# Diffusion step with a DeltaNet layer on one core: the early splits and the second layer's modulation tied to the first MLP's instructions

## The chip, the cores and the metric

The kernel runs on one core of one Trainium2 chip. The metric is the device time of one execution in microseconds (us); lower is better. TensorE is called PE below, VectorE DVE, ScalarE ACT, GpSimd POOL and SyncE SP; SP computes nothing here, its queue issues most of the transfers (DMAs).

## The reference, cut to what matters

Two layers run over 128 context tokens and 512 latent tokens that share the weights: an attention layer and a gated DeltaNet layer. Each is followed by an MLP, and each norm is modulated by vectors that are themselves a product of a condition with a weight matrix:

```python
def modulation(cond, w_mod, b_mod):
    m = jax.nn.silu(cond) @ w_mod + b_mod              # (1024) @ (1024, 6144), per layer and per group
    return jnp.split(m[..., None, :], N_MOD, axis=-1)
def trunk_layer(x, mods, gain1, gain2, w1, w2, mixer):
    shift1, scale1, gate1, shift2, scale2, gate2 = mods
    mix, aux = mixer(rms_norm(x, gain1) * (1 + scale1) + shift1)
    x = x + gate1 * mix
    h = rms_norm(x, gain2) * (1 + scale2) + shift2
    x = x + gate2 * (jnp.square(jax.nn.relu(h @ w1)) @ w2)   # (1024 -> 4096 -> 1024)
    return x, aux
def delta_mixer(h, ...):
    proj = h @ w_in                                    # q, k, v, z: 8 heads of 128 columns each
```

All of it is float32. The kernel makes a product of two float32 matrices from three faster products: each operand is split into a high part (a rounded copy) and a low part (what the rounding left), and high times high, high times low and low times high are added.

## The kernel before, in words

Activations lie transposed, features on the partitions: eight tiles of 128 features by 640 tokens. A dense layer goes through its weight matrix in blocks of 128 output columns and, for each block, through two halves of 320 tokens. One block and one half are 24 matmuls of 128x320 (eight feature tiles, three products each); this unit is called a half step below. The MLP of a layer has four quarters of 8 blocks of `w1` and 8 blocks of `w2`, so 64 blocks and 128 half steps.

A block's weights come by one 512 KB transfer into a `raw` buffer (three of them, filled by SP's queue), and ACT writes the high part and DVE the low part into a pair of `wx` buffers (five pairs). The sink of a `w1` half step is a ReLU on ACT, a product on DVE, and a split on both; that of a `w2` half step is one or two adds to `x` on DVE. Results lie in five PSUM buffers until their sink has run.

While the first MLP runs (`mlp(0, ...)`), two other pieces of work are to be done beside it:

- `modulate(1, 0, ...)`, the product that gives the second layer's first shift and scale. The condition has 32 columns, and `w_mod` streams through PE in 128x512 pieces. Four of them, with `tile_position=(0, 32 * q)` for q from 0 to 3, make one of eight accumulation steps; each writes another 32 partitions of the PSUM tile `mod`. Their weights come into two `raw` buffers of 512 KB each.
- `presplit()`, which splits 29 blocks of the DeltaNet layer's input weights ahead of time. A block comes as two 256 KB pieces into `rawp` (three buffers), ACT writes the high part of a piece and DVE the low part into a pair of `w` buffers (three pairs), and two 512 KB transfers on POOL's queue write the pair to DRAM (`wd`), from where the DeltaNet layer reads it.

All of this is written as Python generators that `weave` interleaves by their numbers of steps. The order in which the engines get the instructions is not that of the code, though: a scheduler with priorities and an assumed duration for each instruction sorts them afterwards, and an instruction of low priority goes ahead wherever the scheduler believes its engine free. Each engine then works strictly in its order, and waits where an operand is missing. The last steps of the MLP (`mid2`) load and split three more pairs of `w` buffers for the DeltaNet layer's first head and normalise the first token half.

Of the kernel before, what the change touches and what calls it, by code (L numbers as in the profile page):

```python
# [15 lines left out]
P = 128  # L16
D = 1024
FT = D // P
# [59 lines left out]
def weave(*parts):  # L78
    live = [[0, n, i, g] for i, (g, n) in enumerate(parts)]
    while live:  # L80
        live.sort(key=lambda e: ((e[0] + 1) / e[1], e[2]))
        e = live[0]
        try:
            next(e[3])
            e[0] += 1
        except StopIteration:
            live.pop(0)


def drain(g):  # L90
    for _ in g:
        pass


class Model:
# [277 lines left out]
    def modulate(self, l, slab, fetch, alloc=None, early=False):  # L373
        nc = self.nc
        acc = alloc or (lambda: self.ps("mod", 1))
        ps = acc()[:, :512]
        get = lambda k: fetch(self.a["w_mod"][l, k * P : (k + 1) * P, slab * 2048 : (slab + 1) * 2048])
        ahead = get(0) if early else None
        for k in range(FT):
            views = ahead or get(k)  # L380
            ahead = get(k + 1) if early and k + 1 < FT else None
            for q in range(4):
                nc.tensor.matmul(  # L383
                    ps[32 * q : 32 * q + 32, :], self.cond[:, k, :], views[q],
                    start=k == 0, stop=k == FT - 1, tile_position=(0, 32 * q),
                )
            yield
        m = self.main("x", shape=[P, 512])
        self.act(m, ps, AF.Copy)
        pt = acc()[:, :512]  # L390
        for b in range(4):
            self.tr(pt[:, b * P : (b + 1) * P], m[:, b * P : (b + 1) * P])
        src = pt.rearrange("p (b q i) -> p q b i", b=4, q=4)
        dst = self.mods[l][:, slab * 16 : slab * 16 + 16, :].rearrange("p (q b) i -> p q b i", q=4)
        bias = self.c1[:, l * 48 + slab * 16 : l * 48 + slab * 16 + 16].rearrange("p (q b) -> p q b", q=4)
        for i in range(2):
            self.tt(dst[:, :, :, i], src[:, :, :, i], bias, ALU.add)
        if slab != 1:
            which = 0 if slab == 0 else 1
            kind = 1 if slab == 0 else 4  # L400
            n = self.c1[:, 96 + 16 * which + 8 * l : 104 + 16 * which + 8 * l]
            for g in range(2):
                self.stt(self.gains[l][which][:, :, g], self.mods[l][:, kind * FT : kind * FT + FT, g],
                         self.one_col, n, ALU.add, ALU.mult)
        yield
# [9 lines left out]
    def fetch_mixed(self, src):  # L415
        r = self.raw([P, 2, 512])
        self.nc.sync.dma_start(out=r, in_=src[:, :1024].rearrange("p (q c) -> p q c", q=2))
        out = [r[:, 0, :], r[:, 1, :]]
        for i in (2, 3):
            t = self.main("a", shape=[P, 512])  # L420
            self.nc.sync.dma_start(out=t, in_=src[:, i * 512 : (i + 1) * 512])
            out.append(t)
        return out

    def fetch_slots(self, src):
        out = []
# [420 lines left out]
    def presplit(self):  # L847
        self.wd = {}
        todo = [(hd, kind) for hd in range(HEADS) for kind in (1, 0, 2) if hd] + [(hd, 3) for hd in range(HEADS)]
        w = self.a["dn_w_in"][0]  # L850
        HK = FT // 2

        def load(t, i):
            r = self.scr("rawp", 3, [P, HK, P])
            c = self.wcol(*t)
            self.nc.sync.dma_start(out=r, in_=w[i * HK * P : (i + 1) * HK * P, c : c + P].rearrange("(k p) c -> p k c", p=P))
            return r

        steps = [(t, i) for t in todo for i in range(2)]
        raws = [load(*x) for x in steps[:2]]  # L860
        for n, (t, i) in enumerate(steps):
            if n + 2 < len(steps):
                raws.append(load(*steps[n + 2]))
            if i == 0:
                pair = self.wtile(), self.wtile()
            ks = slice(i * HK, (i + 1) * HK)
            self.split(raws.pop(0), pair[0][:, ks, :], pair[1][:, ks, :])
            if i == 1:
                name = self.nm("wd")
                d = self.wd[t] = self.dp.tile([2, P, D], F32, tag=name, bufs=1, name=name)  # L870
                for z in range(2):
                    self.nc.gpsimd.dma_start(out=d[z], in_=pair[z].bitcast(F32).rearrange("p k c -> p (k c)"))
            yield
# [392 lines left out]
    def run(self):  # L1266
        tc, nc, a = self.tc, self.nc, self.a
# [3 lines left out]
        with psum("ps0") as self.pq:  # L1271
# [3 lines left out]
            x = []  # L1275
# [7 lines left out]
            h = self.first_norm(x, gm)  # L1283
# [3 lines left out]
        with pool("mlp0") as self.ph, psum("ps3") as self.pq:  # L1287
            self.extra = 3
            x = self.reload(self.xd)
            h = self.new_h()  # L1290
            nxt = []
# [13 lines left out]
                nxt2[:] = [self.pair(w, 0, kind * D) for kind in (1, 0, 2)]  # L1305
                self.mod_norm(x, 1, 0, h2, 0)

            weave((self.mlp(0, h, x, nxt, mid2), 128), (self.modulate(1, 0, self.fetch_raw), 13), (self.presplit(), 64))
            self.mod_norm(x, 1, 0, h2, 1)
            h = h2  # L1310
            xd = self.spill(x, nc.scalar)
# [91 lines left out]
```

## Time and profile before

| | |
|---|---|
| median of 3 runs | 1934.23 us (1922.34 to 1940.01) |
| the profiled execution's own time | 1927.58 us |
| its span, first to last instruction | 1925.6 us |
| PE busy | 1802.5 us (94%), 11981 records |
| DVE, ACT, POOL busy | 987.3, 754.1, 310.0 us |
| mean granted clock of PE | 0.976 |

Times inside the kernel are counted from the start of the span. A float32 matmul on PE leaves two records where a matmul on split operands leaves one. The first MLP's half steps run on PE from 356 to 869 us.

### The profile page before, as it was taken

To read this page: it belongs to the slowest core of one execution; us is meant where nothing else is said; L and a number is where in the kernel's file an instruction comes from. 1 tells how busy PE (TensorE), PEld (TensorE's weight loads), DVE (VectorE), ACT (ScalarE), POOL (GpSimd) and SP (SyncE) were. 2 spreads that over 40 slices of the span, in tenths; PEclk is the share of its full clock that TensorE was granted. 3 is DMA by queue.
4 is the path that set the end of the run, shared out by engine and by line. 5 is a ranking of instruction groups with operands and counts; after the bars stand their busy time and mean duration, and the time that the engine had idled before them with its cause. 6 is when DMAs were issued, how large, how long until landed. Compare 5 with 4: busy or idle time off the path is not lost.

```text
span 1925.6 us, 31049 instructions
## 1 busy us (share of the span) xinstructions
PE 1802.5 (94%) x11981; PEld 1665.9 (87%) x11981; DVE 987.3 (51%) x2293; ACT 754.1 (39%) x1725; POOL 310.0 (16%) x405
## 2 busy tenths in 40 slices
PE   6999999988799999999999999999799999999997
PEld 2777877977789999999888988776699999999997
DVE  4646663744443333455778876653645334343342
ACT  2445542543331322334756655524433223131331
POOL 2343221411100000032211111110232000000012
PEclk8899999999999999999999999999999999999998
DMA  7651147399943332233434233564622222222211
GB/s 274 219 162 35 34 131 218 103 346 346 364 126 120 100 89 76 77 99 126 138 108 117 76 97 112 162 185 150 206 64 77 77 77 75 70 76 77 77 45 55
DMA packets 289065, 248.84 MB, mean 129 GB/s; under 512 B 44847, under 2 KB 246982, under 8 KB 288918
## 3 DMA queue, kind: packets, MB, share of 16 engines
q1 hardware_dynamic: 269072, 207.85, 35.6%
q0 software_dynamic: 9136, 32.18, 4.4%
q10 hardware_dynamic: 10710, 6.83, 1.1%
q8 instruction: 94, 1.54, 0.3%
q14 instruction: 53, 0.43, 0.1%
HBM read 199.00 MB, written 45.20 MB: 127 GB/s over the span
## 4 chain that ended last, share of the span: by engine, by line
PE 67%; DVE 14%; DMA 12%; ACT 3%; issue 2%; POOL 1%; SPq 0%; ACTq 0%; POOLq 0%; DVEq 0%
PE dense L148 28%; PE pd L148 27%; DMA rawp<-in_dn_w_in 5%; PE scan L148 3%; PE big L148 2%; DMA raw<-in_mlp_w 2%; PE pd L383 1%; DVE cv L141 1%; PE mod L383 1%; DVE ptmp L135 1%; PE big L151 1%; DMA ptmp<-gmd 1%; DMA raw<-in_w_mod 1%; DVE wx L135 1%; DVE a L135 1%
## 5 line engine op out<-in xcount | busy, mean ns | idle before, releaser
L148 PE MATMUL pd<-h,w 128*128 128x320 f32 x2016 | 354.0, 320 | 12.0 <-ACT cv L138 7.5
L148 PE MATMUL dense<-a,wx 128*128 128x320 f32 x2238 | 342.4, 312 | 18.2 <-ACT a L138 12.4
L148 PEld LDWEIGHTS dense<-a,wx 128*128 128x128 f32 x2238 | 333.3, 189 | 23.4 <-ACT a L138 13.3
L148 PEld LDWEIGHTS pd<-h,w 128*128 128x128 f32 x2016 | 301.3, 190 | 37.9 <-issue 21.0
L138 ACT ACTIVATE wx<-raw 128x1024 fp32r<-128x1024 f32 x132 | 139.5, 1057 | 361.7 <-PE dense L148 184.8
L148 PE MATMUL dense<-h,wx 128*128 128x320 f32 x1776 | 266.7, 310 | 5.1 <-DVE x L141 2.6
L148 PEld LDWEIGHTS dense<-h,wx 128*128 128x128 f32 x1776 | 263.1, 189 | 5.9 <-issue 3.1
L135 DVE TENSOR_TENSOR wx<-raw,wx 128x1024 fp32r<-128x1024 f32 x127 | 158.5, 1250 | 177.5 <-ACT wx L138 177.2
L148 PE MATMUL pd<-a,wx 128*128 128x320 f32 x1284 | 197.4, 311 | 3.4 <-DVE x L141 2.6
L148 PEld LDWEIGHTS pd<-a,wx 128*128 128x128 f32 x1284 | 191.3, 189 | 7.6 <-issue 6.2
L135 POOL TENSOR_TENSOR x<-x,half 128x320 f32<-128x320 f32 x48 | 52.4, 1091 | 803.0 <-ACT half L138 795.1
L148 PE MATMUL pd<-h,wx 128*128 128x320 f32 x1008 | 155.8, 314 | 7.7 <-DVE x L141 4.0
L148 PEld LDWEIGHTS pd<-h,wx 128*128 128x128 f32 x1008 | 151.8, 192 | 11.8 <-issue 6.1
L141 DVE SCALAR_TENSOR_TENSOR x<-dense,c,x 128x320 f32<-128x320 f32 (+2 forms) x152 | 61.8, 435 | 164.5 <-PE dense L148 164.4
L138 ACT ACTIVATE a<-half 128x320 fp32r<-128x320 f32 x128 | 60.0, 470 | 107.8 <-DVE half L141 107.8
L135 DVE TENSOR_TENSOR a<-half,a 128x320 fp32r<-128x320 f32 x128 | 62.8, 492 | 63.4 <-ACT a L138 63.4
L141 DVE SCALAR_TENSOR_TENSOR cv<-cv,c,cv 128x644 f32<-128x644 f32 x84 | 78.3, 932 | 18.5 <-ACT cv L138 17.4
L141 DVE SCALAR_TENSOR_TENSOR x<-pd,c,x 128x192 f32<-128x192 f32 (+2 forms) x88 | 35.9, 437 | 92.6 <-PE pd L148 92.5
L135 DVE TENSOR_TENSOR w<-rawp,w 128x512 fp32r<-128x512 f32 x58 | 39.8, 690 | 71.0 <-ACT w L138 70.9
L138 ACT ACTIVATE w<-rawp 128x512 fp32r<-128x512 f32 x58 | 36.5, 630 | 94.5 <-DMA rawp<-in_dn_w_in 92.9
L138 ACT ACTIVATE half<-x 128x320 f32<-128x320 f32 x56 | 26.2, 468 | 107.3 <-DVE x L141 106.1
L148 PE MATMUL big<-wide,a 128*128 128x128 f32 x480 | 65.1, 283 | 0.4 <-issue 0.3
(284 smaller groups left out, 2514.1 us busy)
## 6 DMA issues: line engine op xcount, KB each, us to landing
raw<-in_mlp_w SPq DMA_DIRECT2D x128, 512.0 KB
raw<-in_w_mod SPq DMA_DIRECT2D x64, 512.0 KB
wd<-w POOLq DMA_DIRECT2D x58, 512.0 KB, 5.9
w<-wd SPq DMA_DIRECT2D x58, 512.0 KB
rawp<-in_dn_w_in SPq DMA_DIRECT2D x58, 256.0 KB
a<-in_w_mod SPq DMA_DIRECT2D x48, 256.0 KB
raw<-in_attn_w_in SPq DMA_DIRECT2D x12, 512.0 KB
x<-xs SPq DMA_DIRECT2D x16, 320.0 KB
```

The source lines that it names most:

```text
L135: (eng or self.nc.vector).tensor_tensor(out=out, in0=in0, in1=in1, op=op)
L138: self.nc.scalar.activation(out=out, in_=in_, func=func, **kw)
L141: self.nc.vector.scalar_tensor_tensor(out=out, in0=in0, scalar=s, in1=in1, op0=op0, op1=op1)
L148: self.nc.tensor.matmul(out, l, r, start=first, stop=last)
L151: self.nc.tensor.transpose(out, in_, self.ident[:n, :n])
L383: nc.tensor.matmul(ps[32 * q : 32 * q + 32, :], self.cond[:, k, :], views[q], start=k == 0, stop=k == FT - 1, tile_position=(0, 32 * q),)
```

## The change

`modulate_pieces` takes the place of `modulate(1, 0, ...)`: it loads one 128x512 piece of `w_mod` (256 KB) at a time into the `rawp` buffers, two pieces ahead, and issues one of the four column positions in each of its 32 steps; `raw` is left to the MLP. It is followed by `presplit()` in one generator, `beside()`, no longer side by side with it. `pinned` steps the MLP and lets `beside()` advance by at most 98 steps for 128 of the MLP's. After each step of `beside()`, every instruction that it issued on PE, DVE or ACT gets an ordering edge to the MLP's last instruction on the same engine, so that the scheduler may not put it ahead of that one. Transfers on SP's and POOL's queues get no edge. `beside()` has 33 steps of modulation and 58 of splitting, 91 in all.

```diff
+PINNED = tuple(getattr(mybir.EngineType, n) for n in ("PE", "DVE", "Activation"))
+def pinned(tc, main, n, side, m):
+    ...
+    for _ in main:
+        step += 1
+        for i in traced(at):
+            if i.engine in PINNED:
+                last[i.engine] = i.name
+        at = len(traced(0))
+        while done * n < step * m and next(side, True) is None:
+            done += 1
+            for i in traced(at):
+                if i.engine in last:
+                    tc.add_manual_dep(i, last[i.engine], why, reason="paced")
+            at = len(traced(0))
+    drain(side)
...
+    def piece(self):
+        return self.scr("rawp", 3, [P, FT // 2, P])
+
+    def modulate_pieces(self, l, slab):
+        ps = self.ps("mod", 1)[:, :512]
+
+        def load(n):
+            k, q = divmod(n, 4)
+            r = self.piece().rearrange("p k c -> p (k c)")
+            c = slab * 2048 + q * 512
+            self.nc.sync.dma_start(out=r, in_=self.a["w_mod"][l, k * P : (k + 1) * P, c : c + 512])
+            return r
+
+        raws = [load(n) for n in range(2)]
+        for n in range(4 * FT):
+            k, q = divmod(n, 4)
+            if n + 2 < 4 * FT:
+                raws.append(load(n + 2))
+            self.nc.tensor.matmul(
+                ps[32 * q : 32 * q + 32, :], self.cond[:, k, :], raws.pop(0),
+                start=k == 0, stop=k == FT - 1, tile_position=(0, 32 * q),
+            )
+            yield
+        yield from self.modulation(l, slab, ps, lambda: self.ps("mod", 1))
...
-            weave((self.mlp(0, h, x, nxt, mid2), 128), (self.modulate(1, 0, self.fetch_raw), 13), (self.presplit(), 64))
+            def beside():
+                yield from self.modulate_pieces(1, 0)
+                yield from self.presplit()
+
+            pinned(tc, self.mlp(0, h, x, nxt, mid2), 128, beside(), 98)
```

In the order of the built program, ACT in the first quarter of the MLP, where `w1` ends and `w2` begins, reads as follows before (`wx` is the high part of an MLP block, `w` that of a piece of `presplit`, `half` and `a` the sink of a `w1` half step):

```order
L138 ACTIVATE a_3784<-half_4366 128x320
L138 ACTIVATE w_5868<-rawp_5735 128x512
L138 ACTIVATE w_5868<-rawp_5800 128x512
L138 ACTIVATE wx_4714<-raw_4712 128x1024
L138 ACTIVATE w_6007<-rawp_5866 128x512
L138 ACTIVATE w_6007<-rawp_5939 128x512
L138 ACTIVATE w_6163<-rawp_6005 128x512
L138 ACTIVATE w_6163<-rawp_6070 128x512
L138 ACTIVATE wx_4780<-raw_4778 128x1024
```

and so in the changed kernel, on ACT at the same place:

```order
L163 ACTIVATE wx_4612<-raw_4610 128x1024
L163 ACTIVATE half_4347<-dense_913_4322 128x320
L163 ACTIVATE a_3784<-half_4349 128x320
L163 ACTIVATE wx_4674<-raw_4672 128x1024
L163 ACTIVATE wx_4739<-raw_4737 128x1024
L163 ACTIVATE wx_4801<-raw_4799 128x1024
```

All 58 splits of pieces stood in the first quarter, four between two MLP blocks at its end; now none stands there, and they come from half step 43 on. In the third quarter of the changed kernel, ACT has one of them for every one or two half steps:

```order
L163 ACTIVATE half_6079<-pd_6054 128x320
L163 ACTIVATE a_6032<-half_6081 128x320
L163 ACTIVATE w_6087<-rawp_5960 128x512
L163 ACTIVATE wx_6442<-raw_6440 128x1024
L163 ACTIVATE half_6116<-dense_1171_6091 128x320
L163 ACTIVATE a_6032<-half_6118 128x320
L163 ACTIVATE w_6087<-rawp_5999 128x512
```

They are spread over half steps 43 to 117. PE in the first quarter of the MLP, before, has a group of modulation between two half steps (`mod` is its PSUM tile; a row with x2 is two instructions):

```order
L148 MATMUL pd_4076<-h_3010,wx_4073 128x320
L383 MATMUL mod_4107<-raw_4108,c_97 32x512 x2
L383 MATMUL mod_4107<-raw_4110,c_97 32x512 x2
L148 MATMUL pd_4116<-h_2996,wx_4072 128x320
L148 MATMUL pd_4116<-h_2997,wx_4072 128x320
```

and in the changed kernel, PE at the end of that quarter's `w1` blocks:

```order
L173 MATMUL pd_4288<-h_3011,wx_4284 128x320
L173 MATMUL pd_4288<-h_3010,wx_4285 128x320
L471 MATMUL mod_3817<-rawp_4208,c_97 32x512
L173 MATMUL dense_913_4322<-h_2996,wx_4284 128x320
L173 MATMUL dense_913_4322<-h_2997,wx_4284 128x320
```

Eight groups of four column positions stood every ten half steps over the whole MLP; now each of the 32 instructions stands by itself between two half steps, the first after half step 0 and the last before half step 41, with at most two half steps and at least one between them.

## Rows read from the trace of the kernel before

**Rows 1.** The page's 40 slices of 48.1 us: busy tenths, granted clock, GB/s

```profile
PE   6999999988799999999999999999799999999997
...
PEclk8899999999999999999999999999999999999998
...
GB/s 274 219 162 35 34 131 218 103 346 346 364 126 120 100 89 76 77 99 126 138 108 117 76 97 112 162 185 150 206 64 77 77 77 75 70 76 77 77 45 55
```

**Rows 2.** Busy time by stretch of 25 us: us, then each engine's busy us (records)

```profile
core 0: us, PE busy (x) PEld busy (x) DVE busy (x) ACT busy (x) POOL busy (x), PEclk, DMA share, GB/s
425.00:450.00 25.00, 12.48 (x64) 9.95 (x63) 12.59 (x22) 10.52 (x19) 4.79 (x9) 0.73 1.07 360
500.00:525.00 25.00, 18.23 (x109) 17.30 (x108) 11.17 (x19) 7.22 (x11) 4.25 (x8) 0.93 1.07 374
550.00:575.00 25.00, 25.00 (x173) 25.00 (x172) 11.96 (x20) 10.32 (x20) 0.00 (x0) 1.00 0.39 126
```

**Rows 3.** Waits from 375 to 530 us: who for whom, us, times, longest

```profile
ACT w L138 <- DMA rawp<-in_dn_w_in: 92.9, 43, 7.3
...
PE dense L148 <- ACT a L138: 12.4, 3, 7.7
...
PE pd L148 <- DVE x L141: 6.6, 4, 2.5
```

**Rows 4.** DMA queues from 397 to 530 us

```profile
DMA packets 44986, 46.94 MB, mean 353 GB/s; under 512 B 1792, under 2 KB 38083, under 8 KB 44978
```

**Rows 5.** Busy time in three stretches of the first MLP, columns as in Rows 2

```profile
397.00:550.00 153.00, 121.52 (x746) 114.31 (x745) 69.41 (x114) 53.12 (x89) 25.51 (x48) 0.91 0.96 322
550.00:584.07 34.07, 33.30 (x226) 31.78 (x224) 15.56 (x26) 13.93 (x27) 0.00 (x0) 1.00 0.38 120
584.07:848.80 264.73, 264.73 (x1808) 261.55 (x1805) 103.87 (x174) 73.49 (x116) 8.23 (x8) 1.00 0.33 96
```

**Rows 6.** The same for instructions on the tile mod alone: PE, PEld, DVE, ACT

```profile
397.00:550.00 153.00, 3.20 (x24) 0.47 (x24) 0.00 (x0) 0.00 (x0) 0.91 0.96 322
584.07:848.80 264.73, 3.87 (x32) 0.97 (x28) 0.25 (x2) 0.59 (x1) 1.00 0.33 96
```

**Rows 7.** PE in order of time, third quarter: start, us, instruction, records

```profile
615.89 3.67 PE L148 MATMUL pd<-a,wx 128*128 128x320 f32 x24
619.49 1.07 PE L383 MATMUL mod<-raw,c 128*32 128x512 f32 x8
620.49 3.78 PE L148 MATMUL pd<-a,wx 128*128 128x320 f32 x24
624.11 10.70 PE L148 MATMUL dense<-a,wx 128*128 128x320 f32 x72
634.64 1.63 PE L148 MATMUL pd<-a,wx 128*128 128x320 f32 x10
```

**Rows 8.** PE in order of time, the first layer's modulation at the start

```profile
23.37 1.04 PE L383 MATMUL mod<-a,c 128*32 128x512 f32 x2
24.34 0.66 PE L151 MATMUL big<-c,xin 128*128 128x128 f32 x4
24.93 1.05 PE L383 MATMUL mod<-h,c 128*32 128x512 f32 x4
25.91 0.76 PE L151 MATMUL big<-c,xin 128*128 128x128 f32 x5
```

**Rows 9.** An uncrowded 512 KB load: SP's issue, and ACT that waits for it

```profile
353.33 22.40 SPq L187 DMA_DIRECT2D raw<-in_mlp_w  x4
...
358.32 1.06 ACT L138 ACTIVATE wx<-raw 128x1024 fp32r<-128x1024 f32 x1 [3.97 <-DMA raw<-in_mlp_w]
```

**Rows 10.** Splits of pieces: ns min, median, max

```profile
L138 ACT ACTIVATE w<-rawp x58: 614/632/635, 374.7 to 529.3; 128x512 fp32r<-128x512 f32 x58
L135 DVE TENSOR_TENSOR w<-rawp,w x58: 681/692/694, 376.1 to 530.0; 128x512 fp32r<-128x512 f32 x58
```

**Rows 11.** All 58 writes to wd: from issue to landing

```profile
DMA to landing us min/median/max: 3.5/5.9/11.0
```

**Rows 12.** PE in half step 3: idle before, and for whom

```profile
374.29 4.08 PE L148 MATMUL pd<-h,w 128*128 128x320 f32 x26 [0.41 <-POOL h L135]
```

More of the change, by code (lines that the diff above doesn't have):

```diff
@@ L87, in weave @@
             live.pop(0)
+PINNED = tuple(getattr(mybir.EngineType, n) for n in ("PE", "DVE", "Activation"))
+def pinned(tc, main, n, side, m):
+    nc = tc.nc
+    last = {}
+    why = mybir.DependencyInfo(mybir.DependencyClass.NoSync, mybir.DependencyReason.DATA)
+    traced = lambda i: nc.cur_bb.bb.instructions[i:]
+    at = len(traced(0))
+    done = step = 0
+    for _ in main:
[9 more added lines that the diff above has]
+                    tc.add_manual_dep(i, last[i.engine], why, reason="paced")
+            at = len(traced(0))
+    drain(side)
 def drain(g):
@@ L387, in modulate, with modulation @@
             yield
+        yield from self.modulation(l, slab, ps, acc)
+    def modulation(self, l, slab, ps, acc):
         m = self.main("x", shape=[P, 512])
@@ L853, in load @@
         def load(t, i):
-            r = self.scr("rawp", 3, [P, HK, P])
+            r = self.piece()
             c = self.wcol(*t)
```

## Prediction, made before the changed kernel ran

> **What bounds the kernel now.** I read the page's slices first, then stretches of 25 us, then the waits in the worst of them. PE is busy in nine tenths or more of most slices; three slices in a row, from 385 to 530 us, show less than that, and they are the ones in which the transfers run at 346 to 364 GB/s, more than anywhere else [rows 1]. So the kernel is bound by PE, except there. At the finer scale PE is busy for 12.48 us of the 25 from 425 us and for 18.23 of those from 500, with a granted clock of 0.73 and 0.93 (of 2.4 GHz, so partly at 1.2), while the DMA share is at its ceiling; from 550 on PE is full at a clock of 1.00 and the share falls to 0.39 [rows 2]. The waits name the chain: ACT waits 92.9 us for pieces of the DeltaNet weights, and PE waits for sinks that stand behind those splits on ACT and DVE, 12.4 us for the MLP's activations and 6.6 us for buffers that the adds to x free [rows 3]. The cause is volume: 46.94 MB go through in 133 us, 353 GB/s [rows 4]. The scheduler put all 58 splits into the first quarter of the MLP, which needs 58 x 0.79 = 45.6 MB (0.26 MB read and 0.52 written for each piece), and the queues deliver no faster.
>
> **The unit of the sum.** Three undisturbed half steps take 634.64 - 624.11 = 10.53 us, 3.51 each. Two of them with a group of modulation between take 624.11 - 615.89 = 8.22, so a group of four matmuls costs 8.22 - 7.02 = 1.20 us on PE [rows 7].
>
> **Term 1, the burst goes: what PE gets back.** From 397 to 550 us PE leaves 746 records, of which 24 belong to three groups of modulation [rows 5, 6]; the other 722 are 30 half steps of 24 and two at the edges. They should take 30 x 3.51 + 3 x 1.20 = 108.9 us and take 153.0: lost 44.1. From 550 to 584.07 there are nine half steps and one group, 32.8 us of work in 34.07: lost 1.3. From there to 848.80, 1808 records less 32 of mod are 74 half steps; 74 x 3.51 + 3 x 1.20 + 0.4 for four transposes is 263.7 of 264.73, so the MLP without the burst runs at PE's pace within 1 us [rows 5, 6]. The burst therefore costs 45.4 us, lowered clock included.
>
> Does the work that moves fit where it goes? On ACT and DVE a piece costs 0.63 and 0.69 us [rows 10], in a half step of 3.51 us in which those engines are busy for 28 and 39% (73.49 and 103.87 of 264.73 [rows 5]); 58 pieces in 75 half steps are 0.77 in each, 0.5 us more on either. Of transfers, those 75 half steps (263 us) get 45.6 MB of splits and 37.5 block loads of 0.52 MB, 65.3 MB or 248 GB/s, against the 353 of the burst [rows 4]. A piece is loaded once the third before it has been split, so two to three pieces ahead, some 9 us; an uncrowded load of twice the size took 358.32 - 353.33 = 5.0 us [rows 9]. And PE is five blocks of weights and five PSUM buffers away from a late split. I take all 45.4 us as recovered, less 1.5 for waits that I can't see, with bounds of 0 and 10 for those: 10 is a quarter of the loss, which the burst makes with all 58 pieces where the load here is seven tenths of its rate.
>
> **Term 2, the modulation in single matmuls: what PE pays.** Before, the four column positions stand together, and the order shows them now alone between half steps, 32 of them in place of eight groups. What one costs by itself is seen at the start of the kernel. One instruction (two records) holds PE from 23.37 to 24.34, 0.97 us; two instructions (four records) hold it from 24.93 to 25.91, 0.98 us [rows 8]; four hold it from 619.49 to 620.49, 1.00 us [rows 7]. So the positions run at the same time and one costs what four cost. The change pays 32 times what it paid eight times: 24 x 1.20 = 28.8 us, all of it on PE, which has no idle time outside the burst to hide it in. If only the 0.97 counts and nothing around it, it is 32 x 0.97 - 8 x 1.20 = 21.4; that is the lower bound, and a wait for a late piece would be on top. I take 28.8, since the 0.2 us around a group (before its weight load and at the first matmul after it) have no reason to go for one.
>
> The Trainium skill speaks against this part of the change: "TensorE: Matmul & The Clock Gate", Part 3: Packing small matmuls, says that matmuls on different column groups run concurrently, and its table in "Why this matters for your kernels" gives 2.38 times for three of 32 columns by 512. Rows 7 and 8 agree with the first and are stronger than the second. By that figure, carried to four as an estimate (3.2 groups' worth for four alone), the price would be 8 x 1.20 x 2.2 = 21 us and the result 8 us faster than mine.
>
> **Smaller edits.** At the start, modulation now stands between the first half steps, where PE waited 0.41 us for the normalised second half [rows 12]; that wait goes under it. Two block splits move ahead of the squares of the norm on ACT and DVE there; their loads start about 2 us earlier since no 512 KB of modulation lies in their raw buffers. I take nothing for both, bounds -1 and +1. At the end, a new wait: the third weight pair for the DeltaNet layer needs a w buffer that the last split pair frees only when it is in DRAM. The last piece is split after half step 117; 0.63 + 0.69 for the split and 5.9 for the write [rows 10, 11], and until then that pair's split holds ACT, and behind it the squares of the next norm, and DVE, and behind it three blocks' adds to x. PE needs these only after half step 122, 17.6 us after 117, and the pair's own split (1.06 us on ACT [rows 9], and a like one on DVE) and what queued behind take some 4 us. So 5 us are to spare; with the longest write, 11.0 us, none. Nothing, bound 3. POOL and SP: the writes wait on POOL's queue for splits, and the sums of squares stand behind them only at that same end. On SP a piece of modulation waits for the matmul three before it, and block loads stand behind it; by the order they stand 11 to 16 half steps ahead of PE's need, so a wait of one or two half steps on SP reaches nobody.
>
> **The sum.** -45.4 + 1.5 + 28.8 = -15.1 us. From the profiled execution's 1927.6 us that makes 1912.5; the median of the runs shown is 6.6 us higher, and from it the sum is 1919. Since part of that spread may be the burst itself, which depends on DMA, I take the middle: **1916 us**, 0.9% below the median. About 1% is what a measurement of this kernel tells from no change, so this is a gain at the edge of that.
>
> **Rivals.**
> 1. *Modulation costs little alone.* If a single column position among split matmuls needed a quarter of a group, 0.30 us, term 2 would vanish: 1927.6 - 44 = 1884, from the median 1890. For it: nothing in the trace shows one alone in this neighbourhood, and the bounds and the skill's figure lie on its side. Against: rows 8, three counts at one price. With the cases between (the lower bound of term 2, 1905 to 1911, and a burst that costs more in other runs) I give it 0.20.
> 2. *The waits return in another place.* The splits are late all the same, since ACT works in order and a piece's load is issued only three pieces ahead, while 512 KB writes share the DMA engines; at landings of about 9 us ACT would again pace the sinks, and some 10 to 25 of the 45 us would stay: 1922 to 1944. Against: 248 of 353 GB/s. 0.14.
> 3. *PE waits for pieces of modulation: slower than before.* A piece is requested when PE has done the third before it, three to four half steps ahead, at least 10.5 us and three matmuls of 1.2. It decides above a landing of about 13 us: then each round of three pieces stops PE for the excess, 32/3 = 11 rounds. To end 1% above before it has to cost 15 + 19 = 34 us, 3.2 a round, so landings of 16 us: 1947. Against: 5.0 us uncrowded [rows 9], 11.0 the longest write in the burst [rows 11], and blocks of the MLP alone beside it. 0.06.
> 4. *The edges don't move the burst*: excluded by the order, where the splits are spread.
>
> **How the numbers follow.** The forecast (PE-bound MLP, both terms as summed, 1906 to 1922) gets 0.60, rivals 0.20, 0.14 and 0.06. It lies across the line of 1% at 1915; a bit under half of it, and rival 1, are faster: 0.25 + 0.20 = 0.45. Within 1%: the rest of the forecast and most of rival 2, 0.47. Slower: rival 3 and the end of rival 2, 0.08. The range leaves out rival 3, the far end of rival 2 and the extreme of rival 1: 1896 to 1934.
>
> **What the profile after would show.** Right: no slice under 9 tenths between 385 and 530 us and no stretch there above 300 GB/s; ACT's wait for rawp a few us in all; 32 places where PE goes from a half step to two records of mod and on after 0.97 to 1.0 us, so that 41 half steps with modulation take 41 x 3.51 + 32 x 1.20 = 182 us and the rest 3.51 each; the MLP's end 15 us earlier; the DeltaNet stage as long as before. Wrong: PE's half steps more than 3.51 apart in the third quarter, with ACT or DVE waiting for rawp; gaps ahead of mod ended by its load; a gap at the first norm of the DeltaNet layer.

## The result, and the profile after

| | median, us | lowest to highest | runs |
| --- | --- | --- | --- |
| before | 1932.6 | 1922.3 to 1940.0 | 4 |
| after | 1909.7 | 1908.8 to 1910.9 | 4 |

The ratio is 0.9885, 95% interval 0.9839 to 0.9932: faster by 1.15%, and the interval reaches from 0.7 to 1.6%. The profiled execution went from 1927.6 to 1908.8 us, 18.9 less (spans 1925.6 and 1906.9).

The page's slices, now 47.7 us each, in the order of [rows 1]:

```profile
PE   6999999999999999999899999999899999999997
PEclk8899999999999999999999999999899999999999
GB/s 278 219 157 43 34 109 212 103 76 113 102 127 254 227 269 225 257 160 128 129 111 118 81 86 131 167 189 135 224 53 79 70 75 78 78 74 70 78 45 56
```

The three slices at 346 to 364 GB/s are gone, and so are the 8, 8 and 7 of PE that stood there. The same bytes now pass at 225 to 269 GB/s in five slices of the MLP's second half. The three stretches of [rows 5], the last one cut where the MLP now ends:

```profile
397.00:550.00 153.00, 153.00 (x885) 125.94 (x885) 48.48 (x79) 33.80 (x54) 0.00 (x0) 1.00 0.37 105
550.00:584.07 34.07, 34.07 (x235) 33.97 (x234) 18.35 (x34) 14.92 (x27) 3.30 (x6) 1.00 0.53 168
584.07:836.90 252.83, 252.83 (x1725) 252.83 (x1724) 132.12 (x214) 98.93 (x163) 36.69 (x60) 1.00 0.79 245
```

PE has no idle time left in any of them and its granted clock is 1.00, the full 2.4 GHz. In the last one the splits and their writes run beside it: ACT 39% busy, DVE 52%, 245 GB/s, and PE does not notice. The second part of the change is seen in PE's order of time, the MLP's first half steps; columns as in [rows 7]:

```profile
373.97 1.04 PE L471 MATMUL mod<-rawp,c 128*32 128x512 f32 x2
374.95 3.79 PE L173 MATMUL dense<-h,w 128*128 128x320 f32 x24
378.67 1.04 PE L471 MATMUL mod<-rawp,c 128*32 128x512 f32 x2
379.65 3.79 PE L173 MATMUL pd<-h,w 128*128 128x320 f32 x24
383.37 1.04 PE L471 MATMUL mod<-rawp,c 128*32 128x512 f32 x2
```

A half step with a lone modulation matmul has a period of 378.67 - 373.97 = 4.70 us, against 3.51 without: 1.19 for one, where [rows 7] has 1.20 for four. No idle time stands in brackets, so none of these pieces comes late. The waits say the same: of PE in the MLP (362 to 850 us), and of ACT from 530 to 840:

```profile
PE nps L289 <- POOL x L160: 2.5, 1, 2.5
...
ACT w L163 <- DMA rawp<-in_dn_w_in: 39.7, 21, 3.9
```

PE's only wait is at the sums of squares with which the MLP begins. ACT still waits 39.7 us for pieces of weights, 21 times and never over 3.9 us at once, and PE waits for nothing behind it ([rows 3] had 92.9 in 43, up to 7.3, with PE behind).

To price the MLP in each kernel I take the stretch on PE from the first matmul of the sums of squares ahead of it to the first of those at its end; in every kernel the last five half steps stand behind that second mark. Before:

```profile
355.97 0.38 PE L264 MATMUL nps<-c,x 128*128 128x1 f32 x2 [1.23 <-POOL x L135]
...
848.83 0.28 PE L264 MATMUL nps<-c,x 128*128 128x1 f32 x2
```

After:

```profile
362.05 0.58 PE L289 MATMUL nps<-c,x 128*128 128x1 f32 x2 [2.52 <-POOL x L160]
...
836.91 0.28 PE L289 MATMUL nps<-c,x 128*128 128x1 f32 x2
```

It takes 492.9 us before and 474.9 after, 18.0 less. All the rest of the program takes 1925.6 - 492.9 = 1432.7 and 1906.9 - 474.9 = 1432.0. So the change acts where it was made. That the MLP starts 6.1 us later and what follows it is 6.8 us shorter is mostly scatter: over all the kernels below, in which PE has the same work there, its start lies between 350.8 and 362.1 and the stretch behind it between 1068 and 1079 us. The five profiles of kernels that load the modulation in pieces start it late, though, at 357.3 to 362.1, the others at 350.8 to 358.3; 1.3 to 2.5 us of that is a wait that comes up again below. The granted clock has the larger part: its mean ahead of the MLP is 0.98 in the two executions that start it at 350.8 and 351.4, and 0.95 in the one that starts it at 362.1. Two neighbouring windows ahead of the MLP, before:

```profile
305.00:315.00 10.00, 7.82 (x44) 6.46 (x43) 2.02 (x3) 2.58 (x3) 0.93 (x2) 0.83 0.75 225
315.00:325.00 10.00, 9.00 (x57) 7.46 (x57) 5.83 (x8) 4.12 (x5) 2.66 (x2) 1.00 0.76 223
```

and after:

```profile
305.00:315.00 10.00, 7.84 (x48) 4.81 (x46) 2.14 (x3) 1.99 (x3) 1.72 (x2) 0.96 0.66 212
315.00:325.00 10.00, 9.76 (x49) 9.76 (x50) 4.57 (x7) 4.71 (x5) 1.29 (x1) 0.70 0.84 232
```

PE is idle for 2.2 us in the first window of both, and the clock then falls, in these 20 us to a mean of 0.915 before and 0.83 after: some 1.7 us' worth of difference at one place. ACT's order is the same there; the work stands some 3 us later in the second, so this gives a size only.

### The profile page after: what moved, and what is told of

Same layout as the page of the kernel before. It is cut to its first block, busy times and chain, and to the rows that moved or that the text cites. A ratio compares the mean times of both kernels' runs of the same rounds, so it can differ in the third digit from the quotient of the medians.

```text
span 1906.9 us, 31083 instructions
## 1 busy us (share of the span) xinstructions
PE 1816.6 (95%) x11981; PEld 1660.6 (87%) x11981; DVE 990.3 (52%) x2293; ACT 754.5 (40%) x1725; POOL 311.9 (16%) x405
## 4 chain that ended last, share of the span: by engine, by line
PE 75%; DVE 15%; DMA 5%; issue 2%; ACT 1%; POOL 1%; SPq 1%; POOLq 0%; ACTq 0%; DVEq 0%
PE dense L173 33%; PE pd L173 29%; PE scan L173 3%; PE big L173 2%; DVE cv L166 2%; DVE ptmp L160 2%; PE mod L471 2%; PE pd L408 1%; PE mod L408 1%; DVE ptri L1083 1%; PE big L176 1%; DVE wide L160 1%; DVE a L160 1%; DMA ptmp<-gmd 1%; PE S L173 1%
## 5 line engine op out<-in xcount | busy, mean ns | idle before, releaser
L925 POOL DMA_DIRECT2D wd<-w x58 | 31.1, 536 | 398.9 <-ACT w L163 355.1
L166 DVE SCALAR_TENSOR_TENSOR cv<-cv,c,cv 128x644 f32<-128x644 f32 x84 | 78.2, 931 | 20.0 <-ACT cv L163 18.9
L173 PEld LDWEIGHTS big<-wide,a 128*128 128x128 f32 x480 | 58.0, 191 | 5.8 <-ACT a L163 1.7
```

The source lines that it names most:

```text
L166: self.nc.vector.scalar_tensor_tensor(out=out, in0=in0, scalar=s, in1=in1, op0=op0, op1=op1)
L173: self.nc.tensor.matmul(out, l, r, start=first, stop=last)
```

## The experiments

The theory was that of the prediction: the burst's end gives back some 45 us, and 32 single matmuls in place of eight groups take some 29 again. All the kernels in one table; "MLP" is the stretch just defined, in the profiled execution:

| kernel | median, us (runs) | ratio to before, 95% | MLP, us |
| --- | --- | --- | --- |
| before | 1924.8 to 1932.6 (4, 13, 9, 7, 7) | | 492.9 |
| after | 1909.7 (4) | 0.9885 (0.9839 to 0.9932) | 474.9 |
| groups of four, paced | 1878.8 (4) | 0.9771 (0.9739 to 0.9803) | 445.6 |
| pairs | 1891.7 (4) | 0.9837 (0.9804 to 0.9870) | 457.4 |
| four from each piece | 1913.2 (10) | 0.9937 (0.9918 to 0.9956) | 475.1 |
| half the columns | 1893.1 (4) | 0.9858 (0.9817 to 0.9899) | 461.3 |
| groups, pace 133 | 1882.1 (4) | 0.9748 (0.9717 to 0.9778) | 449.6 |
| groups, pace 200 | 1897.7 (4) | 0.9829 (0.9800 to 0.9859) | 467.3 |
| groups paced, splits free | 1939.0 (6) | 1.0056 (1.0032 to 1.0080) | 509.6 |
| splits paced, groups free | 1891.5 (4) | 0.9808 (0.9773 to 0.9843) | 457.4 |
| groups and even splits | 1897.0 (4) | 0.9840 (0.9807 to 0.9872) | 465.2 |
| even splits, pairs | 1880.0 (4) | 0.9757 (0.9717 to 0.9796) | 455.0 |
| after, again | 1907.4 (4) | 0.9885 (0.9848 to 0.9921) | 477.9 |

**Groups of four, paced.** The edges stay, the pieces go.

```diff
             def beside():
-                yield from self.modulate_pieces(1, 0)
+                for _ in self.modulate(1, 0, self.fetch_raw):
+                    for _ in range(4):
+                        yield
                 yield from self.presplit()
```

> The changed kernel with its ordering edges, but with the modulation in eight groups of four matmuls from 512 KB loads through the MLP's raw buffers, as before the change; a group stands at every fourth of the side's steps, so the splits keep their places. Theory (the single matmuls cost 24 x 1.20 us more, all of it on PE): 1909.7 - 28.6 = 1881 us, at most 2 us either way. Rival A (a lone matmul among split matmuls is cheap and the burst was worth only some 18 us): 1909.7, no change. Rival B (two of the three raw buffers are held for each group until PE gets there, and the block loads behind them on the queue come late): PE waits for a split block at up to seven groups, some 3 us each, so about 1900.

It ran in 1878.8 us, with four runs within 0.9 us: 30.8 below the changed kernel, faster than both kernels, and the intervals of the two ratios don't touch. (The two kernels were timed on different occasions; by their ratios to before the distance is 22 us, with some 11 either way.) The MLP is 29.2 us shorter. PE at its ends and at one group:

```profile
357.74 0.28 PE L289 MATMUL nps<-c,x 128*128 128x1 f32 x2
...
397.73 3.68 PE L173 MATMUL dense<-h,wx 128*128 128x320 f32 x24
401.34 1.07 PE L408 MATMUL mod<-raw,c 128*32 128x512 f32 x8
402.34 7.31 PE L173 MATMUL dense<-h,wx 128*128 128x320 f32 x48
...
803.37 0.28 PE L289 MATMUL nps<-c,x 128*128 128x1 f32 x2
```

Eight records, four instructions, hold PE for 1.00 us, where two records, one instruction, held it for 0.98 above. Rivals A and B both fall: PE waits 0.2 us in the whole MLP. The second layer's MLP, which has no modulation and no splits beside it, takes 436.2 us between the same marks (1403.9 to 1840.0) in this execution; with eight groups at 1.20 that is 445.8, and the 445.6 here leaves no loss to find.

**Pairs.** Sixteen stops of two positions, from the same 256 KB pieces:

```diff
-        raws = [load(n) for n in range(2)]
+        raws = [load(n) for n in range(3)]
         for n in range(4 * FT):
             k, q = divmod(n, 4)
-            if n + 2 < 4 * FT:
-                raws.append(load(n + 2))
             self.nc.tensor.matmul(...)
-            yield
+            if n % 2:
+                raws += [load(m) for m in (n + 2, n + 3) if m < 4 * FT]
+                yield
+                yield
```

> The changed kernel with its 256 KB pieces used two at a time: 16 stops of two neighbouring column positions in place of 32 of one, everything else in place. Theory (a stop costs 1.2 us however many positions are in it): 16 x 1.19 = 19.0 us less, 1890.6. Rival (the price goes by the matmul): no change, 1909.7. With two pieces needed at once and a third buffer behind them, a late load would show as PE waiting for rawp: the load of the second piece of a stop can start only when the stop before it is done, two to three half steps earlier, 7 us or more against some 3 to 5 for a landing, so none is expected.

1891.7, 18.0 below the changed kernel; the MLP 17.4 shorter. A pair holds PE from 397.31 to 398.30, 0.99 us, as long as a lone matmul:

```profile
397.31 1.05 PE L469 MATMUL mod<-rawp,c 128*32 128x512 f32 x4
398.30 7.32 PE L173 MATMUL pd<-h,wx 128*128 128x320 f32 x48
```

The price goes by the stop. The median is 1.1 us above the forecast, and PE's order has the reason: it takes the first pair in two parts, at 367.30 and 369.13 us with two records each, so there are 17 stops, and 15 x 1.19 = 17.9.

**Four from each piece.** The opposite: 32 stops, each with four matmuls.

```diff
-            self.nc.tensor.matmul(
-                ps[32 * q : 32 * q + 32, :], self.cond[:, k, :], raws.pop(0),
-                start=k == 0, stop=k == FT - 1, tile_position=(0, 32 * q),
-            )
+            r = raws.pop(0)
+            for p in range(4):
+                self.nc.tensor.matmul(
+                    ps[32 * p : 32 * p + 32, :], self.cond[:, k, :], r,
+                    start=n == 0, stop=n == 4 * FT - 1, tile_position=(0, 32 * p),
+                )
```

> The changed kernel, in which each of the 32 stops multiplies its piece into all four column positions, so four matmuls in place of one; the first modulation of the second layer is not the reference's in it. Theory (the positions run at the same time, 0.97 us for one and 1.00 for four): 32 x 0.03 = 1 us more, 1910.7. Rival (the price goes by the matmul, 0.30 us each): 96 x 0.30 = 29 us more, 1938.

```profile
398.26 1.06 PE L473 MATMUL mod<-rawp,c 128*32 128x512 f32 x8
399.26 7.32 PE L173 MATMUL pd<-h,wx 128*128 128x320 f32 x48
```

96 matmuls more, and the MLP takes 475.1 us in place of 474.9. The two MLPs don't start alike, though: from 357 to 370 us the clock is 0.87 in the changed kernel and 1.00 here. From the three matmuls behind the first sums (`nps<-c,rsy`, at 369.59 and 365.56) to the MLP's end it is 467.3 and 469.0 us, so the 96 matmuls cost 1.7. About 1 of that is the first stop, which PE takes in two parts here; the others have a period of 4.70 to 4.72, in place of 4.70. The run's median is 3.5 above the changed kernel's. The price by the matmul (1938) is out.

**Half the columns.** What of a stop's 1.19 us are the columns (the copy of the result behind it takes these 256 columns twice, in place of 512; that line isn't shown):

```diff
-                ps[32 * q : 32 * q + 32, :], self.cond[:, k, :], raws.pop(0),
+                ps[32 * q : 32 * q + 32, :256], self.cond[:, k, :], raws.pop(0)[:, :256],
```

> The changed kernel, in which each single matmul takes the first 256 of its 512 columns; the other half of the first modulation of the second layer is left out. Theory (the 0.97 us that one holds PE is the passing of 512 columns): half of it goes, 32 x 0.48 = 15.5 us less, 1894. Rival (it is a fixed price of the change of kind among the split matmuls): no change, 1909.7. What is left of the 1.19 us in the trace is the price that doesn't go by columns.

```profile
405.71 0.62 PE L475 MATMUL mod<-rawp,c 128*32 128x256 f32 x2
406.26 3.79 PE L173 MATMUL dense<-h,wx 128*128 128x320 f32 x24
409.98 0.62 PE L475 MATMUL mod<-rawp,c 128*32 128x256 f32 x2
```

The period is 409.98 - 405.71 = 4.27, so 0.43 less than 4.70 for 256 columns fewer, 32 times 13.8; the MLP is 13.6 shorter, the run 16.6 (1893.1). If the first 256 columns cost what the second do, the 512 are 0.86 of the 1.19, and 0.33 goes with the stop. Two widths were measured, so that split is an estimate.

**Pace 133 and pace 200.** How dense may the splits stand? In the kernel with paced groups, one number:

```diff
-            pinned(tc, self.mlp(0, h, x, nxt, mid2), 128, beside(), 98)
+            pinned(tc, self.mlp(0, h, x, nxt, mid2), 128, beside(), 133)   # and 200
```

> The kernel with paced groups of four, the side at 133 steps to 128 half steps in place of 98: the 58 splits now stand in 56 half steps, 1.04 in each in place of 0.77. The transfers of such a half step are 1.04 x 0.79 MB and 0.26 MB of the MLP's own blocks, 1.08 MB in 3.51 us, 308 GB/s, against the 353 that the burst of before went through at. Theory (the loss comes only from a demand above what the queues deliver): nothing is lost, 1879 us, at most 3 more. Rival (it comes from splits standing close before the sinks on ACT and DVE, at any density): some part of the 47 us, about 1890.

> The same with the side at 200 steps to 128 half steps: 1.56 splits in a half step, so 1.56 x 0.79 + 0.26 = 1.49 MB in 3.51 us, 425 GB/s, more than 353. The 58 splits stand in 37 half steps, 130 us, and 55 MB take 157 us at 353 GB/s. Theory (ACT and DVE wait for pieces, and the sinks stand behind them in order): up to 27 us are lost, from 1879 to 1906, the page's GB/s at 340 to 360 for three slices; I expect 15 to 27. Rival (five blocks of weights and five PSUM buffers, ten half steps, hide a lateness of 27 us): 1879 to 1884 with the same GB/s.

At 133 the MLP takes 449.6, 3.9 us more than at 98: two waits of PE, 0.8 and 0.9 us, at 657 us, and a lower clock behind them (0.97 in the 50 us from 635). That is a little more than the 3 us that I had allowed: below the rate of the burst nearly nothing is lost, and the rival's 1890 is not reached (1882.1). At 200 the MLP takes 21.6 us more than at 98, the middle of what was expected, and the run 1897.7. Two windows of it, and PE's two largest waits from 360 to 600 us:

```profile
535.00:560.00 25.00, 14.42 (x81) 13.31 (x82) 16.95 (x27) 13.87 (x27) 5.31 (x10) 0.77 1.01 333
560.00:585.00 25.00, 22.43 (x135) 21.93 (x135) 11.12 (x21) 7.83 (x13) 4.26 (x8) 0.89 1.04 339
...
PE pd L173 <- ACT a L163: 11.8, 3, 7.7
PE dense L173 <- DVE half L166: 2.5, 1, 2.5
```

PE keeps up, but for 1.3 us, for 75 us at 323 to 345 GB/s (460 to 535 us). Then the picture is that of [rows 2, 3]: PE waits for the MLP's activations behind splits on ACT, and the clock falls. What runs out is not the store of five blocks: for split blocks PE waits 1.0 us in all, and 2.5 for a PSUM buffer that a late sink frees. The 11.8 us lie where a quarter goes from `w1` to `w2`: the first half step of `w2` needs the activations of the last ones of `w1`, and blocks in store are of no use there. The 12.4 us of [rows 3] lay at such a place, too. The longest wait of each, pace 200 first, then before:

```profile
556.62 6.42 PE L173 MATMUL pd<-a,wx 128*128 128x320 f32 x24 [7.71 <-ACT a L163]
...
437.88 5.46 PE L148 MATMUL dense<-a,wx 128*128 128x320 f32 x24 [7.72 <-ACT a L138]
```

**Groups paced, splits free.** The edges on the modulation alone, presplit woven in as before the change (stepped is pinned with a yield after every step):

```diff
-                yield from self.presplit()
-            pinned(tc, self.mlp(0, h, x, nxt, mid2), 128, beside(), 98)
+            weave((stepped(tc, self.mlp(0, h, x, nxt, mid2), 128, beside(), 98), 128), (self.presplit(), 64))
```

> The kernel with paced groups of four, the splits without edges again, so that the scheduler places all 58 ahead of the MLP's first dozen of activations, as before the change; the modulation keeps its paced places. Theory (the edges on the splits alone are worth the whole gain): the time before the change, 1925 us on the chip of the last runs, within 6, and a spread between runs of 10 us or more as before has, in place of 1 to 2. Rival (the modulation's order had a part in the burst): clearly under it, 1885 to 1910.

Slower than before, 1939.0, and 8 us beyond the expected 1919 to 1931. With the groups paced, the edges on the splits are worth the whole gain and more. It was not expected that the MLP would be 16.7 us longer than before (509.6). The paced groups stand closer, 5 half steps apart where [rows 6] has three in 153 us, so their loads fall into the burst, and PE waits for them and behind ACT; PE's waits from 360 to 600 us:

```profile
PE dense L198 <- ACT a L188: 9.6, 1, 9.6
PE mod L433 <- DMA raw<-in_w_mod: 7.5, 4, 2.5
PE mod L201 <- ACT x L188: 6.8, 1, 6.8
```

Its six runs lie within 5.4 us, where I expected 10 or more: that the burst as such makes runs scatter is not borne out.

**Splits paced, groups free.** The other part alone, which is the kernel before with edges on its splits:

```diff
             def beside():
-                for _ in self.modulate(1, 0, self.fetch_raw):
-                    for _ in range(4):
-                        yield
+                for _ in range(36):
+                    yield
                 yield from self.presplit()
-            pinned(tc, self.mlp(0, h, x, nxt, mid2), 128, beside(), 98)
+            weave((stepped(tc, self.mlp(0, h, x, nxt, mid2), 128, beside(), 98), 128),
+                  (self.modulate(1, 0, self.fetch_raw), 13))
```

> The kernel before the change with one part of it alone: the splits paced by edges, at the same places as in the changed kernel; the modulation stays in its eight groups of four, 10 half steps apart through the MLP, without edges. Theory (the edges on the splits are worth the whole gain and the single matmuls are all of the price): as with paced groups, 1879, at most 3 either way; the MLP from its first to its last sums of squares 446 us. Rival (the modulation's edges matter too, since two of three raw buffers are held for a group and the loads of later blocks wait): PE waits for split blocks in the paced stretch, 1885 to 1900.

**Groups and even splits.** Both from the first half step on, the splits at 182 GB/s:

```diff
             def beside():
-                for _ in self.modulate(1, 0, self.fetch_raw):
-                    for _ in range(4):
-                        yield
-                yield from self.presplit()
+                g, p = self.modulate(1, 0, self.fetch_raw), self.presplit()
+                for n in range(94):
+                    if n % 4 == 0 and n < 36:
+                        next(g, None)
+                    if (n + 1) * 58 // 94 > n * 58 // 94:
+                        next(p, None)
+                    yield
+                drain(g)
+                drain(p)
```

> The kernel with paced groups of four, the splits spread evenly from the first half step to the 122nd, 0.48 in each, in place of 0.77 from the 48th on: 0.48 x 0.79 + 0.26 = 0.64 MB in 3.51 us, 182 GB/s. Theory (at 248 GB/s nothing is lost any more, so a lower rate has nothing to give): 1879, at most 2 either way. Rival (some part of the burst's price is still there at 248): up to 5 us less. A second rival, on the other side: in the first half steps the splits stand among the normalisation's work on ACT and DVE, PE waits there 1 to 3 us, 1880 to 1882.

Both missed: 1891.5 and 1897.0 in place of 1879, the MLP 11.8 and 19.6 us longer than with the groups ahead of the splits. The rival on record for the first of them (groups hold two of three raw buffers, 1885 to 1900) has the time right. In the second the demand on the queues is lower and the loss greater: this was a wait of another kind. In the even kernel PE's waits from 480 to 550 us are

```profile
PE mod L176 <- ACT x L163: 6.5, 1, 6.5
PE mod L408 <- DMA raw<-in_w_mod: 2.4, 1, 2.4
PE dense L173 <- DVE half L166: 2.3, 1, 2.3
```

and ACT and SP there show why. SP's issues of loads, and under them what ACT then waits for:

```profile
496.80 0.34 SPq L439 DMA_DIRECT2D raw<-in_w_mod  x1
...
498.32 0.46 SPq L439 DMA_DIRECT2D raw<-in_w_mod  x1
498.82 0.42 SPq L212 DMA_DIRECT2D raw<-in_mlp_w  x1
...
511.82 6.74 SPq L212 DMA_DIRECT2D raw<-in_mlp_w  x2
...
509.47 1.06 ACT L163 ACTIVATE wx<-raw 128x1024 fp32r<-128x1024 f32 x1 [9.89 <-DMA raw<-in_mlp_w]
```

Of the three raw buffers a group's two loads take two. The MLP's blocks then go through the one that is left, one at a time: the loads at 483.69, 490.20 and 511.82 are each issued as DVE ends the split of the block before (483.67, 490.18, 511.79). By itself a block then lands after some 4 us (ACT starts on the one of 490.20 at 494.45), but the one issued at 498.82, right behind a group's two loads, takes 10.6 us, and for 13 us (498.82 to 511.82) no load into `raw` is issued. ACT sits 9.9 us at that block, and the split pieces and the sinks stand behind it; from 520.8 us five loads are issued in a heap, and PE, behind ACT's late work, stops. One thing here stays open: PE was done with a group at 484.2 and with the next at 507.2, and the next loads of blocks waited for the one buffer even so, until 490.2 and 511.8.

Without splits on ACT (the paced groups' first 36 steps) the same shortage reaches nobody. With the groups free the last group's two loads, issued at 617.5, hold their buffers until PE comes to them at 646.0, and the blocks go one at a time from 619 to 652; PE waits 5.6 us for ACT's activations between 657 and 669, again where `w1` goes over to `w2`. Some 2 us more go at the MLP's start, as before the change. This is my first run's rival B, in a place where I had not looked for it.

The two parts of the change act together. With the groups paced, the edges on the splits take 64.0 us out of the MLP (509.6 to 445.6), with the groups free 35.5 (492.9 to 457.4). Pacing the groups alone costs 16.7, and gains 11.8 once the splits are paced.

**Even splits, pairs.** The last kernel with 16 stops of two from one 512 KB load each, so that a stop holds one raw buffer:

```diff
+    def modulate_pairs(self, l, slab):
+        ps = self.ps("mod", 1)[:, :512]
+        for n in range(2 * FT):
+            k, i = divmod(n, 2)
+            r = self.raw([P, 2, 512])
+            ...
+            self.nc.sync.dma_start(out=r, in_=src[:, i * 1024 : (i + 1) * 1024].rearrange(...))
+            for j in range(2):
+                ...
+            yield
+        yield from self.modulation(l, slab, ps, lambda: self.ps("mod", 1))
-                g, p = self.modulate(1, 0, self.fetch_raw), self.presplit()
+                g, p = self.modulate_pairs(1, 0), self.presplit()
-                    if n % 4 == 0 and n < 36:
+                    if n % 2 == 0 and n < 36:
```

> The kernel with evenly spread splits, its eight groups of four made into 16 stops of two neighbouring positions, each from one 512 KB load: a stop holds one of the three raw buffers where a group held two. The run before this one lost 20 us in the MLP (465 us from the first to the last sums of squares, against 446 with the groups ahead of the splits). Theory (a group's two buffers leave the MLP's blocks one, they come late, and splits and sinks stand behind them on ACT): the 20 us go or most of them, the eight added stops cost 8 x 1.19 = 9.5 us, so the MLP takes 455 to 460 us and the run 1887 to 1892. Rival (splits among the sinks from the first half step on are the cause): the 20 us stay, 475 us and 1907. A third way: any load of modulation in the rotation of three holds up the third load behind it until PE gets there, so with 16 loads in place of 8 pairs it gets no better: 475 us or more.

The MLP takes 455.0 us, the 455 of the theory, though it runs eight stops more: 445.6 + 8 x 1.19 = 455.1 leaves no wait. PE's stops are undisturbed:

```profile
396.71 1.05 PE L487 MATMUL mod<-raw,c 128*32 128x512 f32 x4
397.69 7.31 PE L173 MATMUL dense<-h,wx 128*128 128x320 f32 x48
404.84 3.68 PE L173 MATMUL pd<-h,wx 128*128 128x320 f32 x24
```

So the group's two loads at a time were the cause, and the splits among the first half steps were not. Pairs halve both what a stop holds of the raw buffers and what it puts ahead of a block in the queues, so which of the two counts is not shown. The median, 1880.0, is better than the 1887 forecast; the profiled execution had a clock of 0.988 and 1419 us outside the MLP, where the others had 1429 to 1436. PE's work is the same there, and why the clock was higher in all four runs (0.986 to 0.988) is not shown.

**After, again.**

> The changed kernel as it is, beside the kernel before on this chip. All theories expect 1910, within 2; the question is how far the comparison itself moves, since before's median was 1933 of four runs on one chip and 1925 to 1929 of 13, 9 and 7 on others: a ratio of 0.989 to 0.993.

1907.4 us against 1930.6, ratio 0.9885 (0.9848 to 0.9921): the first measurement repeated. Its MLP took 477.9, 3.0 more than in the first profile. The window of 13 us around the MLP's start shows where:

```profile
357.00:370.00 13.00, 10.48 (x45) 9.89 (x44) 6.67 (x16) 2.83 (x4) 3.02 (x3) 0.63 0.69 193
```

and in the first profile:

```profile
357.00:370.00 13.00, 10.48 (x59) 9.19 (x58) 8.12 (x17) 2.83 (x4) 4.37 (x4) 0.87 0.72 203
```

PE is equally busy in both but gets through 45 records in place of 59, at a clock of 0.63 in place of 0.87; (0.87 - 0.63) x 13 = 3.1 us. The 2.5 us wait at the sums of squares lies in these windows. From 370.28 us in the first profile and 371.85 in this one, where the same half step starts, both take 466.6 us to the MLP's end, so the whole difference lies ahead of that.

## Why the prediction was right

It said 1916, in a range of 1896 to 1934, and 1909.7 and 1907.4 were measured. The forecast itself held, with both its terms.

*Term 1, the burst goes.* Summed to 45.4 less 1.5. With the modulation in groups on either side, both parts paced, it measures 492.9 - 445.6 = 47.2 us (35.5 where the groups stay free and meet the paced splits). It was 3.3 too small: the 1.5 for unseen waits were not needed, since PE waited for nothing in the MLP; and the first half step of the MLP before had two waits, 1.6 us for squares and the 0.4 of [rows 12], that I left under the smaller edits at nothing. The argument for fitting (248 of 353 GB/s) holds at that density and at 308 but for 3.9 us, and fails at 425, as the two paces show. Its last support, five blocks and five PSUM buffers between a late split and PE, does not hold where `w1` goes over to `w2`, as pace 200 shows.

*Term 2, single matmuls.* 28.8, measured 29.2 in the MLP, and 32.2 in the second profile of the changed kernel. The lower clock at the MLP's start is in these: of the 29.2 it has about (1.00 - 0.87) x 13 = 1.7 us, so the stops took some 27.5. The step by which it was found, that a position costs what four cost [rows 7, 8], is shown by three edits: 16 stops give back 17.4, four matmuls in each stop add 1.7 (with one stop in two parts), and half the columns give back 13.6. The Trainium skill's rule, "TensorE: Matmul & The Clock Gate", Part 3: Packing small matmuls, that matmuls in different column groups run concurrently, agrees with that. Its 2.38 times for three, from the table in "Why this matters for your kernels", does not carry over: here four in place of one hold PE for 1.00 us in place of 0.98, so grouping gains nearly fourfold, and the price of 21 us worked out from that figure is out.

*Smaller edits.* Taken at nothing, and they come to about nothing, of two parts that I had not seen. In the MLP the 2.0 us above are won. Ahead of it the sums of squares wait 2.5 us for POOL in place of 1.2 (the rows at the top), in each kernel with the pieces; with groups of four and edges they don't, or for 0.5 at most. I had noted that two splits of blocks move ahead of the norm's squares on ACT and DVE, and should have charged for it. DVE's splits of blocks right ahead of the last adds to `x` that these squares need are two before and three after:

```profile
349.64 3.67 DVE L135 TENSOR_TENSOR wx<-raw,wx 128x1024 fp32r<-128x1024 f32 x2
...
354.47 5.48 DVE L160 TENSOR_TENSOR wx<-raw,wx 128x1024 fp32r<-128x1024 f32 x3
```

In the kernel with paced groups none stands there, and PE has no such wait. The price is 1.3 us, and a lower clock behind it in four of the five profiles. At the end no wait shows, as forecast.

*The sum.* -15.1 forecast, -18.0 in the MLP and -18.9 in the profiled execution. On the profiled scale 1912.5 was said and 1908.8 came, 3.7 less, which is term 1's shortfall (3.3) and little else. The medians differ by 23.0 and 23.3, since before's profiled execution lies 3 to 5 us below its medians on those chips; the 1919 from the median was 9 to 12 too high for that reason on top, and 1916 stood between.

*Rivals.* 1, cheap lone modulation: out. 2, the waits return: not in the change, but it is what pace 200 and the two kernels with overlapped groups show, for two different reasons. 3, PE waits for pieces: no such wait. 4, the edges don't move the burst: out.

*What the profile would show.* Right were the slices, the transfers and the period of 4.70. The MLP's end comes 11.9 us earlier, not 15, since the MLP began 6.1 later; it is 18.0 shorter. What follows is 6.8 us shorter, not equal, within the scatter. Wrong was "ACT's wait for rawp a few us in all": it is 39.7, and harmless, since each is under 4 us and PE waits for nothing behind it.

Not settled: why the clock outside the MLP, where the executions take 1419 to 1436 us, differs between them, and why the blocks keep to one raw buffer after PE is done with a group.

## What to carry to other kernels

Look for two prices in a change that moves work to a better place: here the move itself was worth 47 us and the smaller pieces that went with it cost 29, and either could be read from a few rows of the trace before it ran. Matmuls that fill one column position of four should be issued four at a time, since here a stop cost the same for one as for four. Before long-lived loads share a small set of buffers with a stream, count how many of the buffers they hold while another engine gets to them, how much they put ahead of the stream's next load, and what stands in order behind that load. A store of blocks does not cover a late engine where the next product needs the last results of the one before: there the lateness reached PE at once.

## What was not expected of the hardware

The 13 us around a wait of 2.5 us on PE had a granted clock of 0.87 in one execution of the changed kernel and of 0.63 in another; the second took 3 us more for the same instructions. In a third kernel with the same wait, four from each piece, it stayed at 1.00. And lower demand on the transfers was no safety: at 182 GB/s the MLP lost 19.6 us, at 425 GB/s 21.6, by way of a group's two loads in the one and of the queues' rate in the other.
